# Last chunk of the input projection: sums of cb and gate tiles by accumulating transfers too, convolution and gating a block later, feed forward's sum cleared two blocks sooner

## The chip, the cores and the metric

The kernel runs on one core of a Trainium2 chip. The metric is the device time of one execution in microseconds. Before the change it is 1202.89 us, the median of three runs (1202.86 to 1203.3). The engines of the core are named as the profile names them: PE is TensorE (matrix products; PEld its weight loads), DVE is VectorE, ACT is ScalarE, POOL is GpSimd and SP is SyncE. Each runs its own list of instructions in order and waits on semaphores for the others.

## The reference, cut to what matters

One decoder layer on 256 rows of 2048 elements, float32. An input projection `proj = h @ w_in` gives eight parts; a gated short convolution (cb, cc, cx) and a gated linear attention (q, k, v, its decay, and the gate r) use them, the two results side by side go through `w_out`, and a feed-forward with its own convolution follows.

```python
def hybrid_mixer(h, w_in, conv_w, gate_w2, gate_b, gla_norm_w, w_out):
    proj = h @ w_in
    cb, cc, cx, q, k, v, r, a_lr = jnp.split(proj, splits, axis=-1)
    y_conv = cb * causal_dwconv3(cc * cx, conv_w)
    log_a = jax.nn.log_sigmoid(a_lr @ gate_w2 + gate_b) / GATE_TAU
    o = gla_chunked(q, k, v, log_a)
    o = rmsnorm(o, gla_norm_w) * jax.nn.silu(r)
    return jnp.concatenate([y_conv, y_gla], axis=-1) @ w_out

mod = c_act @ w_mod + b_mod
sh_m, sc_m, g_m, sh_f, sc_f, g_f = jnp.split(mod, 6)
h = rmsnorm(x, mix_pre_w) * (1 + sc_m) + sh_m
x = x + g_m * rmsnorm(hybrid_mixer(h, ...), mix_post_w)
h = rmsnorm(x, ffn_pre_w) * (1 + sc_f) + sh_f
x = x + g_f * rmsnorm(conv_ffn(h, ...), ffn_post_w)
```

cb, cc and cx are 1024 columns each, q and k 512 each, v and r 1024 each. The six rows of `mod` are products of one vector with a 2048 by 12288 matrix.

## The kernel before, in words

Every matrix product is made of three: both factors are split into a high part and the small rest, and high·high, high·low and low·high are added up in PSUM. For weights this costs, per tile, a load of `raw` (SP queue), a cast to `wh` on ACT (L140) and a subtraction to `wl` on DVE (L145).

The work is a list of units, each with one weight tile of about 1 MB. `drive` writes the order out by hand: for unit i first the steps in its list `early`, then the load and the cast of unit i+2, the `wl` of unit i+1, the steps in `pre`, the products of unit i on PE (after its first tile the steps in `inner`), the steps in `mid`, the evacuations of unit i−1, and the steps in `late`. What is written down first runs first on its engine, so these lists are the schedule.

The input projection goes over its contraction in four chunks. A chunk's units cover all output columns; sums over the chunks are kept in SBUF. In the first chunk a finished PSUM tile is copied there, in the second and third DVE adds PSUM to it. In the fourth, the last, there are two ways. By one, DVE adds as before (L477 for column tiles of 128x512, L494 for row tiles of 128x384 or 128x256). By the other, for the names in `BY_DMA` (cc, cx and v), ACT copies PSUM to a tile `hf` (L474, L491), of which there are three buffers, and POOL starts a DMA that adds `hf` into the sum in SBUF (L475, L492). Column pair 10, the first pair of cx1, is left out of the second way.

`tail` lists the last chunk's 18 units and then the 16 units of the out-projection, so tail[18] is the first of those. The chunk's order is k, v, cc/cx/cb (tail[6] to tail[14]) and the gate r (tail[15] to tail[17], three, three and two column tiles of each half, r0 and r1 being the two halves of the rows). The tables of numbers in the diff are places in `tail`:

- `CONV` puts the four pairs of the convolution: cc·cx (L668 on DVE), the first tap (L673 on ACT), four taps and the product with cb (L136 and L680 on DVE), and the split into high (L684 on ACT) and low (L688 on DVE).
- `SILU` puts the two halves of silu of r (L893 on ACT, after a table load).
- `GATE` puts, for the four heads, the product with the gate (`gated`, L868 on DVE, in `pre`), the transposes on PE (`turn`, L874, in `late`), and a unit later the scaled copies (L880 on ACT, L136 on DVE), which are the left factors of the out-projection's later units.

The linear attention's result comes out of PSUM by L861 (ACT) after its row norms (L401, L851).

An out unit is 24 products of 512 columns (L913, L914, L915) into four PSUM banks that stay in use over eight units; there are eight banks in all.

The rows of `mod` are summed on DVE, step by step, in a tile `macc` of 128x2048 (L136, one step per MB of `w_mod`). A sum begins on POOL with a memset of `macc` (L174) and a small DMA of the bias (L175). Its end is a product with ones on PE (L355, into four banks) which DVE takes from there (L360). `f1` is the sum for the feed-forward's shift and scale: 17 steps, of which the first is the begin, spread over early and mid places of units from `MODS[3]` = 48 (tail[7]) on; the units tail[12], [13], [16] and [17] are left out. L355 and L360 at about 375 us are of the sum before it, used after the out-projection.

Of the kernel before, what the change touches and what calls it, by code (L numbers as in the profile page):

```python
# [24 lines left out]
CHUNKS = (2, 4, 5, 5)  # L25
# [10 lines left out]
NBIG = 20  # L36
XLD = (4, 8)
NLD = (9, 13)
GATE = (18, 19, 20, 21)
SILU = (17, 18)  # L40
CONV = (9, 12, 13, 15)
MODS = (10, 22, 33, 48, 72)
CHUNK1 = 12
BUSY_TAIL = (12, 13, 16, 17)
BY_DMA = ("cc", "cx", "v")
F2_AT = (71, 74, 16)
FULL = ()
FULL1 = ()
# [19 lines left out]
def spread(steps, units, last=()):  # L68

    places = [p for u in units for p in ((u.early, u.mid, u.late) if u in last else (u.early, u.mid))]  # L70
    for i, f in enumerate(steps):
        places[i * len(places) // len(steps)].append(f)
# [31 lines left out]
def layer_kernel(ctx: ExitStack, tc, x, c, w_mod, b_mod, mix_pre_w, mix_post_w, w_in, conv_w, gate_w2, gate_b,  # L104
# [14 lines left out]
    def nm(s):  # L119
        uid[0] += 1  # L120
        return f"{s}_{uid[0]}"

    def slot(shape, dt=F32):
        return big.tile(shape, dt, tag="big", name=nm("big"))
# [7 lines left out]
    def raw_tile(shape):  # L132
        return wts.tile(shape, F32, tag="raw", name=nm("raw"), bufs=NRAW)

    def stt(o, a, s, b, op0=ALU.mult, op1=ALU.add):
        nc.vector.scalar_tensor_tensor(o, a, s, b, op0=op0, op1=op1)  # L136
# [24 lines left out]
    def mod_steps(s0, n, a, w, nj, lag=0):  # L161

        accs, cur, rows = [], {}, []

        def use(j, r):
            stt(cur["acc"], r, c_act[:, j:j + 1], cur["acc"])

        def begin():  # L170
            acc = cur["acc"] = (slot([P, n, w]) if n * w <= 1024 else
                                wts.tile([P, n, w], F32, tag="macc", name=nm("macc"), bufs=2))
            accs.extend(acc[:, s, :] for s in range(n))
            nc.gpsimd.memset(acc, 0.0)  # L174
            nc.gpsimd.dma_start(acc[0:1, :, :], b_mod_v[:, s0:s0 + n, a:a + w])  # L175

        def step(j):
            if j >= KT:
                use(*rows.pop(0))
                return  # L180
            m = nj if j < KT - nj or nj < 4 else 2
            if j % m == 0:
                cur["r"] = raw_tile([P, m, n, w])
                if m == 1:
                    nc.sync.dma_start(cur["r"][:, 0, :, :], w_mod_v[:, j, s0:s0 + n, a:a + w])
                else:
                    for s in range(n):
                        nc.sync.dma_start(cur["r"][:, :, s, :], w_mod_v[:, j:j + m, s0 + s, a:a + w])
            rows.append((j, cur["r"][:, j % m, :, :]))
            if j >= lag:  # L190
                use(*rows.pop(0))

        return accs, [begin] + [lambda j=j: step(j) for j in range(KT + lag)]
# [241 lines left out]
    def hf_tile():  # L435
        return wts.tile([P, 2, T], F32, tag="hf", name=nm("hf"), bufs=NHF)
# [24 lines left out]
    def evac(ci, pair, ps):  # L461

        name = names[pair // 2]
        if name not in proj:
            proj[name] = slot([P, 4, T])
        dst = proj[name][:, (pair % 2) * 2:(pair % 2) * 2 + 2, :]
        if pair not in written:
            written.add(pair)
            nc.scalar.activation(dst, ps, AF.Copy, scale=QS if name == "q" else 1.0)
        elif name == "q":  # L470
            stt(dst, ps, QS, dst)
        elif ci == len(CHUNKS) - 1 and name[:-1] in BY_DMA and pair != 10:
            away_sum = hf_tile()
            nc.scalar.copy(away_sum, ps)  # L474
            nc.gpsimd.dma_start(dst, away_sum, accum_op=ALU.add)  # L475
        else:
            nc.vector.tensor_add(dst, dst, ps)  # L477

    def evac_rows(ci, tiles, t, ps):
# [7 lines left out]
        if ci == 0:  # L487
            nc.scalar.copy(dst, ps)
        elif ci == len(CHUNKS) - 1 and name[:-1] in BY_DMA:
            away_sum = hf_tile().rearrange("p a t -> p (a t)")[:, :w]  # L490
# [64 lines left out]
    def in_units(ci):  # L555
# [18 lines left out]
        def unit(tiles, plain, by_parts=False):  # L574
# [72 lines left out]
            def fin():  # L647
                for p in dict.fromkeys(nt // 2 for nt in tiles):
                    done[p] = done.get(p, 0) + sum(nt // 2 == p for nt in tiles)
                    if done[p] == 2 and p not in keep:  # L650
                        evac(ci, p, banks[p])
# [10 lines left out]
    def conv_pair(i):  # L662

        s = slice((i % 2) * 2, (i % 2) * 2 + 2)

        def first():
            cb, cc, cx = (proj[n + str(i // 2)][:, s, :] for n in ("cb", "cc", "cx"))
            nc.vector.tensor_mul(cc, cc, cx)  # L668

        def tap():  # L670
            cc, cx = (proj[n + str(i // 2)][:, s, :] for n in ("cc", "cx"))
            for j in range(2):
                nc.scalar.activation(cx[:, j, :], cc[:, j, :], AF.Copy, scale=conv_c(2, 2 * i + j))  # L673

        def second():
            cb, cc, cx = (proj[n + str(i // 2)][:, s, :] for n in ("cb", "cc", "cx"))
            for tap, d in ((1, 1), (0, 2)):
                for j in range(2):
                    stt(cx[:, j, d:], cc[:, j, :T - d], conv_c(tap, 2 * i + j), cx[:, j, d:])
            nc.vector.tensor_mul(cb, cb, cx)  # L680

        def high_part():
            mts[i] = slot([P, 2, 2, T], F32R)
            nc.scalar.copy(mts[i][:, :, 0, :], proj["cb" + str(i // 2)][:, s, :])  # L684

        def third():
            cb = proj["cb" + str(i // 2)][:, s, :]
            nc.vector.tensor_sub(mts[i][:, :, 1, :], cb, mts[i][:, :, 0, :].bitcast(F32))  # L688

        return first, tap, second, high_part, third  # L690
# [199 lines left out]
    def gate_silu(g):  # L890
        for t in range(2):
            r = proj[f"r{t}"][:, g * 512:(g + 1) * 512]
            nc.scalar.activation(r, r, AF.Silu)  # L893
# [331 lines left out]
    allin = [u for c in chunks for u in c] + owait  # L1225
# [32 lines left out]
    for h in range(2):  # L1258
        owait[r0 + R0 + 1].mid.append(lambda h=h, f=ones_rows: f(h))
        owait[r0 + R0 + 2].late.append(lambda h=h, f=rows_used: f(h))  # L1260
    f1, fsteps = mod_steps(3, 2, 0, 1024, 1)
    spread(fsteps, [u for i, u in enumerate(allin) if MODS[3] <= i < MODS[4] and i - ends[2] not in BUSY_TAIL])
    for place, f in seconds:
        place.append(f)
# [29 lines left out]
    for g in range(2):  # L1294
        tail[SILU[g]].late.append(lambda g=g: gate_silu(g))
    for e in range(4):
        tail[GATE[e]].pre.append(lambda e=e: gated(e))
        tail[GATE[e]].late.append(lambda e=e: turn(e))
        tail[GATE[e] + 1].pre.append(lambda e=e: weighted(e))
        tail[GATE[e] + 1].late.append(lambda e=e: weighted_low(e))  # L1300
    for i, u in enumerate(CONV):
        first, tap, second, high_part, third = conv_pair(i)
# [220 lines left out]
def build(nc, tc_args=None, arrays=None):  # L1523
    import concourse.tile as _tile

    args = []
    for name, a in arrays.items():
        args.append(nc.dram_tensor(f"in_{name}_dram", a.shape, mybir.dt.from_np(a.dtype), kind="ExternalInput").ap())
    for i, (shape, dtype) in enumerate(_OUTS):
        args.append(nc.dram_tensor(f"out_{i}_dram", shape, getattr(mybir.dt, dtype), kind="ExternalOutput").ap())  # L1530
    with _tile.TileContext(nc, **(tc_args or {})) as tc:
        with tc.manual_schedule():
            layer_kernel(tc, *args)
# [13 lines left out]
```

## Time and profile before

| what | value |
|---|---|
| median of three runs | 1202.89 us (1202.86 to 1203.3) |
| the profiled execution | 1203.08 us |
| its span, from first to last instruction | 1201.1 us |
| busy in the span | PE 97%, DVE 78%, ACT 48%, POOL 4% |
| granted TensorE clock, mean | 0.998 |
| input projection's last chunk | about 250 to 344.7 us |
| out-projection's first product | 344.68 us |

The profile is one execution. A timeline row has the start, the duration, the engine, the line, the tiles and sizes, and in brackets the idle time just before it and what ended that. A row of the chain of waits has start, duration and the work or wait that it stands for; "issue" is time in which the engine waited for nothing that the profile shows. In the groups by line the count is followed by busy time, mean duration of one in ns, and idle time before with its releaser. Buffer numbers are left out of names: `big<-hf` is any of the accumulating transfers.

### The profile page before, as it was taken

The page shows a single profiled execution, that of the slowest core. Times are in us where ns is not written, and L with a number is a line of the kernel's source. Part 1 is how long each engine was busy: PE and PEld are TensorE (multiplying, and loading weights), DVE is VectorE, ACT ScalarE, POOL GpSimd, SP SyncE. Part 2 cuts the span into 40 slices and gives each one's busy share as a digit, 9 for nine tenths or more (in the row PEclk, how much of TensorE's full clock was granted, in tenths as well). Part 3 has the DMA queues.
Part 4 walks back from the last instruction along what each step waited for, and adds up shares of the span by engine and source line. Part 5 has one row for each costly group of instructions (what it writes and reads, how often), then busy time and mean ns, then how long its engine had stood idle before and what let it go on. Part 6 is the DMA issues. An engine that isn't in the chain of part 4 may idle for free.

```text
span 1201.1 us, 16724 instructions
## 1 busy us (share of the span) xinstructions
PE 1166.5 (97%) x6771; PEld 1027.6 (86%) x6771; DVE 939.5 (78%) x963; ACT 576.7 (48%) x671; POOL 47.8 (4%) x66
## 2 busy tenths in 40 slices
PE   3899999999999999999999999999999999999997
PEld 2799999999987888888888888888888888888885
DVE  6979999999999868984698979797976664545463
ACT  4663433463683556445455444544544544343442
POOL 3000110011101010000000000000000000000000
PEclk9999999999999999999999999999999999999999
DMA  9999999998899969995476777668563675555522
GB/s 340 387 361 378 331 383 393 388 330 272 240 341 372 367 248 333 378 369 212 168 260 213 258 259 249 223 243 293 201 236 140 228 263 201 185 202 184 207 73 71
DMA packets 129182, 323.62 MB, mean 269 GB/s; under 512 B 8550, under 2 KB 35894, under 8 KB 119377
## 3 DMA queue, kind: packets, MB, share of 16 engines
q1 hardware_dynamic: 124704, 312.63, 72.2%
q0 software_dynamic: 4256, 9.92, 3.0%
q8 instruction: 53, 0.87, 0.3%
q14 instruction: 25, 0.20, 0.0%
q10 hardware_dynamic: 144, 0.01, 0.0%
HBM read 315.45 MB, written 4.19 MB: 266 GB/s over the span
## 4 chain that ended last, share of the span: by engine, by line
PE 57%; issue 30%; DVE 5%; DMA 5%; ACT 1%; SPq 1%; POOL 1%; POOLq 0%; DVEq 0%; ACTq 0%
PE ps L1057 27%; PE ps L1059 14%; PE ps L913 3%; PE ps L915 3%; PE ps L914 3%; DVE wl L145 1%; DMA big<-hf 1%; PE ps L640 1%; PE ps L639 1%; DVE macc L136 1%; PE ps L638 1%; DMA raw<-in_w_mod_dram 1%; DMA big<-in_w_in_dram 1%; DMA raw<-in_w_in_dram 1%; DMA big<-in_w_mod_dram 1%
## 5 line engine op out<-in xcount | busy, mean ns | idle before, releaser
L140 ACT CAST wh<-raw 128x2048 fp32r<-128x2048 f32 (+2 forms) x200 | 366.3, 1833 | 498.3 <-PE ps L1057 187.3
L145 DVE TENSOR_TENSOR wl<-raw,wh 128x2048 fp32r<-128x2048 f32 (+2 forms) x200 | 437.4, 2190 | 144.7 <-ACT wh L140 144.6
L1057 PE MATMUL ps<-big,wh 128*128 128x512 f32 x1400 | 495.0, 399 | 0.0
L1059 PE MATMUL ps<-big,wl 128*128 128x256 f32 x1400 | 393.1, 281 | 0.0
L1057 PEld LDWEIGHTS ps<-big,wh 128*128 128x128 f32 x1400 | 263.0, 188 | 64.8
L1059 PEld LDWEIGHTS ps<-big,wl 128*128 128x128 f32 x1400 | 264.5, 189 | 0.0
L136 DVE SCALAR_TENSOR_TENSOR macc<-raw,c_act,macc 128x2048 f32<-128x2048 f32 (+1 forms) x96 | 199.3, 2076 | 4.5 <-DMA raw<-in_w_mod_dram 2.2
L913 PE MATMUL ps<-wh,big 128*128 128x512 f32 x456 | 178.4, 391 | 0.0
L915 PE MATMUL ps<-wh,big 128*128 128x512 f32 x456 | 177.5, 389 | 0.0
L914 PE MATMUL ps<-wl,big 128*128 128x512 f32 x456 | 177.5, 389 | 0.0
L640 PE MATMUL ps<-big,wl 128*128 128x256 f32 x504 | 143.3, 284 | 4.6 <-DVE wl L145 4.6
L638 PE MATMUL ps<-big,wh 128*128 128x256 f32 x504 | 143.8, 285 | 0.0
L639 PE MATMUL ps<-big,wh 128*128 128x256 f32 x504 | 142.6, 283 | 0.1
L640 PEld LDWEIGHTS ps<-big,wl 128*128 128x128 f32 x504 | 96.5, 192 | 5.9 <-DVE wl L145 5.8
L915 PEld LDWEIGHTS ps<-wh,big 128*128 128x128 f32 x456 | 85.6, 188 | 18.0
L913 PEld LDWEIGHTS ps<-wh,big 128*128 128x128 f32 x456 | 85.6, 188 | 17.9 <-issue 0.2
L914 PEld LDWEIGHTS ps<-wl,big 128*128 128x128 f32 x456 | 85.6, 188 | 17.6 <-issue 0.2
L639 PEld LDWEIGHTS ps<-big,wh 128*128 128x128 f32 x504 | 96.6, 192 | 0.3 <-DVE big L433 0.3
L638 PEld LDWEIGHTS ps<-big,wh 128*128 128x128 f32 x504 | 96.6, 192 | 0.4 <-ACT wh L140 0.3
L136 DVE SCALAR_TENSOR_TENSOR big<-big,fcw,big 128x254 f32<-128x254 f32 (+1 forms) x176 | 72.1, 475 | 0.0
L983 DVE TENSOR_TENSOR big<-big,ps 128x256 f32<-128x256 f32 x88 | 31.1, 415 | 46.5 <-ACT big L981 46.5
L604 PE MATMUL ps<-wl,big 128*128 128x384 f32 (+2 forms) x168 | 57.1, 340 | 1.2 <-DVE wl L145 1.2
(222 smaller groups left out, 914.0 us busy)
## 6 DMA issues: line engine op xcount, KB each, us to landing
raw<-in_w_up_dram SPq DMA_DIRECT2D x88, 1024.0 KB, 5.1
raw<-in_w_mod_dram SPq DMA_DIRECT2D x64, 1024.0 KB, 6.9
raw<-in_w_down_dram SPq DMA_DIRECT2D x44, 1024.0 KB, 4.8
raw<-in_w_in_dram SPq DMA_DIRECT2D x26, 960.0 KB, 8.0
raw<-in_w_mod_dram SPq DMA_DIRECT2D x32, 640.0 KB, 7.9
raw<-in_w_out_dram SPq DMA_DIRECT2D x16, 1024.0 KB, 7.5
raw<-in_w_in_dram SPq DMA_DIRECT2D x12, 1024.0 KB, 9.1
raw<-in_w_mod_dram SPq DMA_DIRECT2D x22, 512.0 KB, 8.4
```

Source lines behind the costliest of these rows:

```text
L136: nc.vector.scalar_tensor_tensor(o, a, s, b, op0=op0, op1=op1)
L140: nc.scalar.copy(hi, raw)
L145: nc.vector.tensor_sub(lo, raw, hi.bitcast(F32))
L604: nc.tensor.matmul(ps, ht[:, 0, :], w[1][:, kk, :], start=False, stop=kk == n - 1)
L638: nc.tensor.matmul(ps, w[0][:, kk, cs], ht[:, k % 2, 0, :], start=st, stop=False)
L639: nc.tensor.matmul(ps, w[0][:, kk, cs], ht[:, k % 2, 1, :], start=False, stop=False)
L640: nc.tensor.matmul(ps, w[1][:, kk, cs], ht[:, k % 2, 0, :], start=False, stop=sp)
L913: nc.tensor.matmul(ps, a[:, i, 0, ts_], w[0][:, kk, ns], start=st, stop=False)
L914: nc.tensor.matmul(ps, a[:, i, 0, ts_], w[1][:, kk, ns], start=False, stop=False)
L915: nc.tensor.matmul(ps, a[:, i, 1, ts_], w[0][:, kk, ns], start=False, stop=sp)
L1057: nc.tensor.matmul(pss[o], wh[:, kk, cs], h2[k // 2][:, k % 2, :, :], start=(first and kk == 0), stop=False)
L1059: nc.tensor.matmul(pss[o][:, 1, :], wl[:, kk, cs], h2[k // 2][:, k % 2, 0, :], start=False, stop=(last and kk == 3))
```

## The change

cb and r join the names whose last sums go by DMA, and pair 10 is no exception any more: five sums at L477 and six at L494 become a copy on ACT and a DMA of POOL each. The places of gating, silu and convolution move back by one unit each. The begin of `f1` (memset and bias) is taken out of the spread steps and put at the end of tail[5]; the remaining 16 steps are spread over the same places.

```diff
-GATE = (18, 19, 20, 21)
-SILU = (17, 18)
-CONV = (9, 12, 13, 15)
+GATE = (19, 20, 21, 22)
+SILU = (18, 19)
+CONV = (10, 13, 14, 16)
...
-BY_DMA = ("cc", "cx", "v")
+BY_DMA = ("cb", "cc", "cx", "v", "r")
...
-        elif ci == len(CHUNKS) - 1 and name[:-1] in BY_DMA and pair != 10:
+        elif ci == len(CHUNKS) - 1 and name[:-1] in BY_DMA:
             away_sum = hf_tile()
             nc.scalar.copy(away_sum, ps)
             nc.gpsimd.dma_start(dst, away_sum, accum_op=ALU.add)
...
-    f1, fsteps = mod_steps(3, 2, 0, 1024, 1)
+    f1, (f_begin, *fsteps) = mod_steps(3, 2, 0, 1024, 1)
+    allin[MODS[3] - 2].late.append(f_begin)
     spread(fsteps, [u for i, u in enumerate(allin) if MODS[3] <= i < MODS[4] and i - ends[2] not in BUSY_TAIL])
```

Three places show how the order moves. The first is ACT at the turn from the last chunk to the out-projection. `big_511` and `big_513` are the sums of r0 and r1, `ps_...` a PSUM tile, `hf_...` one of the three buffers, `wh_...` a cast weight tile. Before:

```order
L684 CAST big_3445<-big_337 128x2x256
L140 CAST wh_3449<-raw_3447 128x2048
L893 ACT_TABLE_LOAD
L893 ACTIVATE big_511<-big_511 128x512
L893 ACTIVATE big_513<-big_513 128x512
L140 CAST wh_3495<-raw_3493 128x2048
```

With the change:

```order
L491 COPY hf_3447<-ps_3342 128x384
L491 COPY hf_3450<-ps_3358 128x384
L673 ACTIVATE big_483<-big_415,sv 128x256 x2
L140 CAST wh_3459<-raw_3457 128x2048
L491 COPY hf_3500<-ps_3415 128x384
L491 COPY hf_3503<-ps_3431 128x384
L684 CAST big_3506<-big_337 128x2x256
L140 CAST wh_3510<-raw_3508 128x2048
L491 COPY hf_3545<-ps_3468 128x256
L491 COPY hf_3548<-ps_3484 128x256
L893 ACT_TABLE_LOAD
L893 ACTIVATE big_511<-big_511 128x512
```

Six copies now stand among the casts and ahead of the silu, and the silu is one cast later. hf_3503 is the fourth of the six copies; with three buffers it takes the place of hf_3447.

The second place is PE in the out-projection, where the products of the mod rows (L355) stand. Before, the list goes from an out unit to L355 and to the next out unit:

```order
L913 MATMUL ps_3504<-wh_3588,big_3547 128x512
L914 MATMUL ps_3504<-wl_3636,big_3547 128x512
L915 MATMUL ps_3504<-wh_3588,big_3547 128x512
L355 MATMUL ps_3710<-macc_1910,ones 128x512
L355 MATMUL ps_3712<-macc_1910,ones 128x512
L355 MATMUL ps_3714<-macc_1910,ones 128x512
L355 MATMUL ps_3716<-macc_1910,ones 128x512
L913 MATMUL ps_3501<-wh_3634,big_3592 128x512
```

With the change:

```order
L915 MATMUL ps_3517<-wh_3598,big_3602 128x512
L355 MATMUL ps_3725<-macc_1910,ones 128x512
L355 MATMUL ps_3727<-macc_1910,ones 128x512
L355 MATMUL ps_3729<-macc_1910,ones 128x512
L355 MATMUL ps_3731<-macc_1910,ones 128x512
L874 MATMUL ps_3735<-ident,big_3405 128x128
L874 MATMUL ps_3735<-ident,big_3410 128x128
L874 MATMUL ps_3735<-ident,big_3405 128x128
L874 MATMUL ps_3735<-ident,big_3410 128x128
L913 MATMUL ps_3514<-wh_3647,big_3651 128x512
```

The transposes of the fourth head (L874) stood one out unit ahead of L355 and now stand right behind it.

The third place is POOL at v's last transfers (`big_563`, `big_565`). Before:

```order
L492 DMA big_563<-hf_2656 128x384
L492 DMA big_565<-hf_2659 128x384
L492 DMA big_563<-hf_2735 128x256
L492 DMA big_565<-hf_2738 128x256
L174 MEMSET macc_2744 128x2048
L175 DMA macc_2744<-in_b_mod_dram 1x2x1024
```

With the change:

```order
L492 DMA big_563<-hf_2656 128x384
L492 DMA big_565<-hf_2659 128x384
L174 MEMSET macc_2662 128x2048
L175 DMA macc_2662<-in_b_mod_dram 1x2x1024
L492 DMA big_563<-hf_2738 128x256
L492 DMA big_565<-hf_2741 128x256
```

The memset and the bias now go ahead of v's third pair of transfers.

## The prediction, on record before the changed kernel's time was known

> **What bounds the kernel now.** First the busy times on the page.
>
> ```profile
> PE 1166.5 (97%) x6771; PEld 1027.6 (86%) x6771; DVE 939.5 (78%) x963; ACT 576.7 (48%) x671; POOL 47.8 (4%) x66
> ```
>
> TensorE is busy 97% of 1201.1 us, so only the places where it stands still can be gained. The view by windows of 10 us over the last chunk and the start of the out-projection (columns: PE, PEld, DVE, ACT and POOL busy, with counts; granted clock; DMA share; GB/s) shows where these are.
>
> ```profile
> 290.00:300.00 10.00, 9.54 (x81) 9.34 (x80) 10.00 (x11) 3.64 (x5) 0.00 (x0) 1.00 0.70 240
> 310.00:320.00 10.00, 8.10 (x69) 7.89 (x69) 9.97 (x15) 6.73 (x13) 0.85 (x1) 1.00 0.99 314
> 340.00:350.00 10.00, 9.86 (x59) 8.54 (x57) 9.96 (x11) 9.67 (x15) 0.00 (x0) 1.00 0.80 289
> 350.00:360.00 10.00, 9.55 (x46) 7.54 (x45) 10.00 (x13) 6.34 (x8) 0.00 (x0) 1.00 0.99 384
> ```
>
> In each, DVE is full while PE is not, at a granted clock of 1.00. The timeline of PE gives the four stalls to a hundredth.
>
> ```profile
> 294.26 0.28 PE L639 MATMUL ps<-big,wh 128*128 128x256 f32 x1
> 295.00 0.39 PE L640 MATMUL ps<-big,wl 128*128 128x256 f32 x1 [0.46 <-DVE wl L145]
> ...
> 314.96 0.28 PE L639 MATMUL ps<-big,wh 128*128 128x256 f32 x1
> 317.14 0.39 PE L640 MATMUL ps<-big,wl 128*128 128x256 f32 x1 [1.90 <-DVE wl L145]
> 317.37 0.28 PE L638 MATMUL ps<-big,wh 128*128 128x256 f32 x1
> 317.49 0.28 PE L639 MATMUL ps<-big,wh 128*128 128x256 f32 x1
> ...
> 340.50 0.34 PE L604 MATMUL ps<-wl,big 128*128 128x384 f32 x1
> 340.98 0.39 PE L602 MATMUL ps<-wh,big 128*128 128x256 f32 x1
> ...
> 344.68 0.40 PE L913 MATMUL ps<-wh,big 128*128 128x512 f32 x1
> ...
> 349.92 0.39 PE L915 MATMUL ps<-wh,big 128*128 128x512 f32 x1
> 350.75 0.88 PE L874 MATMUL ps<-ident,big 128*128 128x128 f32 x4 [0.45 <-DVE big L868]
> 351.39 0.48 PE L913 MATMUL ps<-wh,big 128*128 128x512 f32 x1
> ```
>
> Back to back, 256 columns follow each other by 0.12 us (317.37 to 317.49). The first two steps take 0.74 and 2.18, so 0.62 and 2.06 are lost, both to wl (L145) coming late from DVE. By the same reckoning 0.31 is lost at 340.98 (0.48 against some 0.17 for 384 columns), and 0.60 at 350.75 (0.83 against 0.23: a unit's 24 matmuls take 349.92 + 0.23 − 344.68 = 5.47). Together **3.6 us**: a ceiling, 0.3% of the time.
>
> **The change part by part.** I call S the start of the out-projection (344.68 before) and follow the terms in the order of the program.
>
> *Work leaving DVE.* The groups by line between 200 and 440 us (count, then busy time and mean ns):
>
> ```profile
> L494 DVE TENSOR_TENSOR big<-big,ps 128x384 f32<-128x384 f32 (+1 forms) x14 | 6.3, 491 | 0.0
> L477 DVE TENSOR_TENSOR big<-big,ps 128x512 f32<-128x512 f32 x8 | 5.3, 676 | 0.4 <-PE ps L640 0.4
> L491 ACT COPY hf<-ps 128x384 f32<-128x384 f32 (+1 forms) x6 | 2.4, 439 | 3.5 <-DMA big<-hf 3.5
> L868 DVE TENSOR_TENSOR big<-big,big 128x256 f32<-128x256 f32 x8 | 3.0, 420 | 0.0
> L893 ACT ACTIVATE big<-big 128x512 f32<-128x512 f32 x4 | 2.3, 624 | 1.7 <-DVE big L494 1.7
> ```
>
> Five sums at L477 and six at L494 leave DVE: 5×0.68 + 6×0.49 = 6.3 us by durations. ACT, idle 3 to 6 us in each window but that of 340 to 350, takes eleven copies, POOL eleven DMA starts. Of these sums two stand ahead of the 2.06 stall, and the convolution's L668, four taps and L680 in its neighbourhood go a block later; I take both stalls on wl as gone. The 0.31 stall ends with L861's first results on ACT, which come sooner because L673 and its wait no longer stand ahead (rows below). The 0.60 stall goes because its transposes go two units later. Term **−3.6 us**; the floor of the gain is zero, if DVE uses the freed time to wait for landings.
>
> *f1's sum cleared sooner.* The chain of waits, at v's last transfers and the memset:
>
> ```profile
> 266.08 7.12 DMA big<-hf
> ...
> 273.58 0.38 ACT hf L491
> 273.96 0.28 issue
> 274.25 0.85 POOL big L492
> 275.10 1.82 POOL macc L174
> ...
> 280.39 2.24 issue
> ```
>
> DVE stood 2.24 us at 280.39, its first sum into macc waiting for the bias behind this memset. Memset and bias now go ahead of v's third transfers, so the bias is down some 7 us sooner and that wait goes. The first macc sum now stands ahead of a wl instead of behind it, and its duration (2.35 in the rows further below) is about the 2.24 saved. PE needs that wl at about the time it then comes: **+0.1**, at most the 0.6 that PE lost to wl at 295. The spread has one step less, because the begin step stands apart; the work is the same.
>
> *The gate's rows by transfer.* This is the long chain. The views of ACT and of the DMA (issues, KB each, median us to landing; the smallest, median and largest of all thirteen):
>
> ```profile
> 337.49 0.91 ACT L673 ACTIVATE big<-big,sv 128x256 f32<-128x256 f32 x2 [1.10 <-DVE big L668]
> 340.10 3.01 ACT L861 ACTIVATE big<-ps,grs 128x256 f32<-128x256 f32 x8
> ...
> big<-hf POOLq DMA_DIRECT2D x4, 192.0 KB, 7.6
> DMA to landing us min/median/max: 3.9/7.0/9.4
> ```
>
> L861 ends at 343.1, or S−1.6. Without the 1.10 wait it ends near S−2.5. The first two copies of the gate (r0, then r1, first three tiles) stand right behind it: a copy of 0.44 and 0.28 to POOL put the first transfer's start at S−1.7. There are three hf buffers. The fourth copy (r1, second three tiles) therefore waits for the first transfer to land, exactly as v's copy did at 273.58: from 266.08 to the next start at 274.25 that hop took 8.17. So the fourth transfer starts at S+6.5, lands 7.6 later at S+14.1, and the silu over both rows (L893, second of its pair) may only then begin: 0.38 for the wake and start as at 273.58, 0.62 of silu, 0.42 of L868, make S+15.6 with 0.1 of signal. Gating a block later lets PE do two units first, 2×5.47, to S+11.0. PE stands **+4.6 us** at the first transposes (L874). What ACT holds behind the blocked copy are the casts of two more blocks of w_out (L140); what DVE holds behind L868 are the next macc sum and wl. PE waits for the same L868 anyway, so these delays are inside the 4.6.
>
> Put generally the stall is (the two landings together) − 10.1. With 3.9 for each it is nothing; with 9.4 for each it is 8.7. I take 7.12 and 7.6, the rows nearest in size and in DMA load: the windows at 310 and 350 have a DMA share of 0.99, that between them 0.80.
>
> [...]
>
> *The fourth transposes behind the mod rows.* Rows of PE and DVE in the out stage of before:
>
> ```profile
> 374.78 3.60 PE L355 MATMUL ps<-macc,ones 128*128 128x512 f32 x8
> 377.81 0.79 PE L913 MATMUL ps<-wh,big 128*128 128x512 f32 x1
> ...
> 351.61 2.35 DVE L136 SCALAR_TENSOR_TENSOR macc<-raw,c_act,macc 128x2048 f32<-128x2048 f32 x1
> 353.87 2.29 DVE L145 TENSOR_TENSOR wl<-raw,wh 128x2048 fp32r<-128x2048 f32 x1
> ...
> 357.53 2.34 DVE L136 SCALAR_TENSOR_TENSOR macc<-raw,c_act,macc 128x2048 f32<-128x2048 f32 x1
> 379.08 2.48 DVE L360 TENSOR_TENSOR big<-ps,big 128x512 f32<-128x512 f32 x4
> ```
>
> The four sums of the out-projection hold four PSUM banks and L355's products the other four. Before, the last L874 ran a unit ahead of L355; now it comes directly behind and needs a bank, which the first L360 on DVE gives back. Call E the end of the stall above. A unit of PE with its transposes is 5.47 + about 0.5, so three of them and L355 (3.03, from 374.78 to 377.81) bring PE there at E+21.0. DVE does macc, wl, L868 and the weighted part per unit in 5.92 (351.61 to 357.53), three times, then a wl (2.2), a macc (2.26) and one L360 (0.62): E+22.9, and 0.1 of signal. **+2.0 us**. It is there only because DVE starts level with PE at E; DVE so far ahead that L360 needn't wait would need 2 us of slack at L868. Bounds: 0 and 2.4.
>
> Sum: −3.6 + 0.1 + 4.6 + 2.0 = **+3.1 us**. At 97% over the whole span PE has no slack behind it that would give this back. The profiled execution took 1203.08 (span 1201.1 and 2.0 around it), 0.2 above the median of 1202.89. Its 1206.2 is 1206.0 for the median.
>
> **The rivals.** *The transfers land early.* At 4.5 us each (9.0 together) PE never waits at the first L874, DVE has 1.1 in hand and the bank costs 0.9: −3.6 + 0.1 + 0.9 = −2.6, time 1200.3, faster. For it: the shortest landing, 3.9. Against: it needs under 5.05 each, two thirds of the median. [...]
>
> *Middle landings.* At 6.2 each: stall 2.3, bank 2.0, sum +0.8, time 1203.7, no change that can be told. For it: the spread of the thirteen is as wide as that. Against: the load of DMA around S.
>
> *The transfers meet the loads of w_out.* The chain of waits has one such, near the end of the chunk, and the timeline of DVE the wait that it made:
>
> ```profile
> 327.77 8.90 DMA big<-hf
> ...
> 336.76 0.69 DVE L668 TENSOR_TENSOR big<-big,big 128x512 f32<-128x512 f32 x1 [1.59 <-DMA big<-hf]
> ```
>
> With 8.9 for each the stall is 17.8 − 10.1 = 7.7 and the sum +6.2: 1209.1. For it: this is the latest landing before S, in a window as full. Against: it carried 256 KB.
> [...] The trace shows only that landings vary from 3.9 to 9.4, not why.
>
> *The change doesn't do what it says:* DVE loses the sums but waits instead for cb to land at L680, and the 3.6 stay. With the terms of the gate that is +6.7, 1209.6. For it: the 1.59 that L668 waits for a landing, just above. Against: the convolution goes a block later, which gives each transfer some 5 us more.
>
> **How the numbers follow.** Chances: forecast 0.42, early landings 0.20, middle 0.20, meeting w_out 0.12, cb late 0.06. A measurement of this kernel can tell about 0.2%, or 2.4 us, from no change: 1200.5 to 1205.3. Early landings are nearly all below that (0.18 faster, 0.02 not). The middle case, and a quarter of the forecast's (landings a little under 7), are inside: 0.20 + 0.11 + 0.02 = 0.33. Slower is 0.49. The range runs from the early case's middle, 1200.3, to 1209.6; it leaves out half of the early case and a part of the long landings, some 2 in 10. The forecast's own range is 1204.5 to 1207.5.
>
> **What would show it.** In the changed kernel's profile: no wait of L640 on wl between 285 and 320; L491 with twelve copies and one of the later ones waiting for the landing of hf; L893 waiting for big<-hf instead of L494; PE waiting at L874 for L868 for some 4.6 us about 10 us into the out-projection, and some 2 us more right behind L355. If the landings of the gate's transfers are near 5 us, or the first L893 waits for nothing, the third and fourth terms are wrong. If L640 still waits for wl, or DVE idles at L668 and L680, the first is wrong. If the last L874 follows L355 without a gap although the first one stood, the bank's term is wrong.

## The result, and the profile after

The changed kernel takes 1206.46 us (median of seven runs, 1205.97 to 1208.1) against 1202.86 us before (seven runs): a ratio of 1.0031, 95% interval 1.0019 to 1.0042. It is slower by 3.6 us; forecast were 3.1. The profiled execution took 1206.61 us, its span is 1204.8.

The page of the changed kernel, part 1, and its view by windows of 10 us (columns as before the change):

```profile
PE 1167.3 (97%) x6771; PEld 1028.6 (85%) x6771; DVE 934.9 (78%) x952; ACT 580.9 (48%) x682; POOL 57.3 (5%) x77
...
290.00:300.00 10.00, 10.00 (x88) 10.00 (x88) 10.00 (x11) 3.41 (x5) 0.85 (x1) 1.00 0.88 233
310.00:320.00 10.00, 10.00 (x87) 10.00 (x86) 9.75 (x14) 6.99 (x15) 3.42 (x4) 1.00 1.08 309
350.00:360.00 10.00, 5.71 (x24) 4.52 (x23) 5.30 (x4) 5.77 (x9) 2.85 (x4) 0.90 1.04 318
```

DVE has eleven operations less, ACT and POOL eleven more. The hole at 310 to 320 us, where PE had been busy 8.10 of 10, is closed. A new one is open at 350 to 360: PE 5.71 of 10, at a mean granted clock of 0.90. The timeline of PE shows what it is.

```profile
287.67 0.28 PE L639 MATMUL ps<-big,wh 128*128 128x256 f32 x1
288.40 0.39 PE L640 MATMUL ps<-big,wl 128*128 128x256 f32 x1 [0.46 <-DVE wl L145]
...
342.44 0.40 PE L913 MATMUL ps<-wh,big 128*128 128x512 f32 x1
...
353.35 0.27 PE L874 MATMUL ps<-ident,big 128*128 128x128 f32 x1
357.90 0.78 PE L874 MATMUL ps<-ident,big 128*128 128x128 f32 x3 [4.29 <-DVE big L868]
358.34 0.77 PE L913 MATMUL ps<-wh,big 128*128 128x512 f32 x1
358.91 0.63 PE L914 MATMUL ps<-wl,big 128*128 128x512 f32 x1
359.33 0.63 PE L915 MATMUL ps<-wh,big 128*128 128x512 f32 x1
...
361.47 0.41 PE L914 MATMUL ps<-wl,big 128*128 128x512 f32 x1
361.72 0.40 PE L915 MATMUL ps<-wh,big 128*128 128x512 f32 x1
...
377.25 3.60 PE L355 MATMUL ps<-macc,ones 128*128 128x512 f32 x8
380.91 0.66 PE L874 MATMUL ps<-ident,big 128*128 128x128 f32 x4
```

The out-projection starts at 342.44 instead of 344.68, 2.2 us sooner. Then PE waits at the first transposes from 353.35 to 357.90. The first seven products behind that wait follow each other by 0.42 to 0.43 us (358.91 to 359.33) where 0.23 is usual, some 1.4 us in all. From L355 to the last transposes it is 3.66 us, where 3.03 would do: 0.6 lost. The feed-forward's first product comes 3.2 us later than before, the span is 3.7 longer; where the other 0.5 arises was not traced.

The chain that makes the long wait, in the timelines of ACT, POOL and DVE:

```profile
339.75 0.90 ACT L491 COPY hf<-ps 128x384 f32<-128x384 f32 x2
343.09 0.53 ACT L491 COPY hf<-ps 128x384 f32<-128x384 f32 x1
347.44 0.48 ACT L491 COPY hf<-ps 128x384 f32<-128x384 f32 x1 [3.82 <-DMA big<-hf]
356.76 0.63 ACT L893 ACTIVATE big<-big 128x512 f32<-128x512 f32 x1 [4.02 <-DMA big<-hf]
...
340.56 1.75 POOL L492 DMA_DIRECT2D big<-hf  x2 [10.28 <-ACT hf L491]
348.21 0.86 POOL L492 DMA_DIRECT2D big<-hf  x1 [3.44 <-ACT hf L491]
...
357.42 0.43 DVE L868 TENSOR_TENSOR big<-big,big 128x256 f32<-128x256 f32 x1 [4.22 <-ACT big L893]
...
380.16 2.48 DVE L360 TENSOR_TENSOR big<-ps,big 128x512 f32<-128x512 f32 x4
```

The first of r's transfers starts at 340.56. The fourth copy of r waits 3.82 us for it to land, since there are three hf buffers, and its own transfer starts at 348.21. The silu waits 4.02 for that one, L868 for the silu and PE for L868. The last row is the product on DVE that gives back the bank for PE's transposes at 380.91.

### The profile page after: what moved, and what is told of

Its sections match the earlier page's. It is cut to its first block, busy times and chain, and to the rows that moved or that the text cites. A ratio compares the mean times of both kernels' runs of the same rounds, so it can differ in the third digit from the quotient of the medians.

```text
span 1204.8 us, 16755 instructions
## 1 busy us (share of the span) xinstructions
PE 1167.3 (97%) x6771; PEld 1028.6 (85%) x6771; DVE 934.9 (78%) x952; ACT 580.9 (48%) x682; POOL 57.3 (5%) x77
## 4 chain that ended last, share of the span: by engine, by line
PE 82%; DVE 5%; DMA 5%; issue 4%; ACT 1%; SPq 1%; POOL 1%; DVEq 0%; POOLq 0%; ACTq 0%
PE ps L1057 27%; PE ps L1059 14%; PE ps L914 8%; PE ps L915 8%; PE ps L913 8%; PE ps L640 3%; PE ps L639 3%; PE ps L638 3%; DMA raw<-in_w_mod_dram 2%; PE ps L603 2%; PE ps L602 2%; PE ps L604 2%; DVE macc L136 1%; DVE wl L145 1%; DMA big<-in_w_mod_dram 1%
## 5 line engine op out<-in xcount | busy, mean ns | idle before, releaser
L640 PE MATMUL ps<-big,wl 128*128 128x256 f32 x504 | 143.1, 284 | 2.7 <-DVE wl L145 2.7
L640 PEld LDWEIGHTS ps<-big,wl 128*128 128x128 f32 x504 | 96.6, 192 | 3.6 <-DVE wl L145 3.5
```

The lines of the kernel that those rows point to most:

```text
L640: nc.tensor.matmul(ps, w[1][:, kk, cs], ht[:, k % 2, 0, :], start=False, stop=sp)
```

## The experiments

Each kernel was timed in five rounds (5 to 11 executions) beside the kernel before, whose medians were 1202.82, 1203.05 and 1203.09 us in the three groups of four runs. Ratios are to those, with 95% intervals.

**r's sums back on DVE.**

```diff
-BY_DMA = ("cb", "cc", "cx", "v", "r")
+BY_DMA = ("cb", "cc", "cx", "v")
```

> The changed kernel with r's last sums back on DVE (L494); gating, silu and all else as changed. Theory (two transfers in a row, tied by the three hf buffers, hold silu and so the first transposes): the 4.3 us wait of PE at the first L874 goes, with it the 1.4 us in which PE ran at a lower granted clock behind it; the wait behind L355 may stay at 0.6 or grow to 2. DVE takes six sums of 0.48 back, in a stretch (320 to 350 us) where it idles some 4 us. Time 1200.5 to 1202.5. Rival (the extra copies and transfers in the chunk, cb's too, take the time by contention): at least 1205.

Measured: 1199.55 us, ratio 0.9974 (0.9964 to 0.9984). It is faster than before, by more than was expected of it. The timeline of PE in this run:

```profile
341.49 0.40 PE L913 MATMUL ps<-wh,big 128*128 128x512 f32 x1
...
352.40 0.60 PE L874 MATMUL ps<-ident,big 128*128 128x128 f32 x4
...
370.21 3.60 PE L355 MATMUL ps<-macc,ones 128*128 128x512 f32 x8
373.96 0.66 PE L874 MATMUL ps<-ident,big 128*128 128x128 f32 x4 [0.16 <-DVE big L360]
```

PE comes to the first transposes 10.9 us into the out-projection and does not wait. The gap between L355 and the last L874 stays at 0.7. So six transfers of r cost 6.9 us of 1206.46, and everything else in the change together gains 3.3.

**Only r1 back on DVE.**

```diff
-        elif ci == len(CHUNKS) - 1 and name[:-1] in BY_DMA:
+        elif ci == len(CHUNKS) - 1 and name[:-1] in BY_DMA and name != "r1":
             away_sum = hf_tile().rearrange("p a t -> p (a t)")[:, :w]
```

> The changed kernel with only r1's last sums back on DVE; r0 keeps its three transfers, one for each hf buffer. Theory (it is the hop over the third buffer that is late): no copy of r waits for a landing of r, the second r0 transfer starts near the out-projection's start and lands some 8 us behind it, ahead of PE's 11; the wait at the first L874 is under 1 us; time 1200.5 to 1202.5, as with all of r on DVE. Rival (one transfer of r is late enough by itself, or DMA load is what counts): a wait of 2 us or more stays, time 1203.5 or more.

Measured: 1202.52 us, ratio 0.9995 (0.9986 to 1.0004), just outside what the theory allowed. For the long wait the theory holds: without the hop over the third buffer no copy of r waits, and the first L874 goes without a stop at 352.62. (This run also halves the number of r's transfers; more buffers with all six were not tried.) But rows of ACT, DVE and PE show what the rest of the time went to:

```profile
354.67 1.15 ACT L893 ACTIVATE big<-big 128x512 f32<-128x512 f32 x2 [2.02 <-DMA big<-hf]
...
358.39 0.88 DVE L136 SCALAR_TENSOR_TENSOR big<-ps,sv,big 128x256 fp32r<-128x256 f32 x2 [1.54 <-ACT big L880]
...
376.22 1.11 PE L874 MATMUL ps<-ident,big 128*128 128x128 f32 x4 [2.23 <-DVE big L360]
376.99 0.78 PE L913 MATMUL ps<-wh,big 128*128 128x512 f32 x1
377.56 0.63 PE L914 MATMUL ps<-wl,big 128*128 128x512 f32 x1
377.99 0.63 PE L915 MATMUL ps<-wh,big 128*128 128x512 f32 x1
```

The second silu waits 2.02 us on ACT for the last transfer. Behind it on ACT stand a cast and L880. DVE waits 1.54 for L880, comes that much later to L360, and PE stands 2.23 at the last transposes, with slow products (0.43 apart) behind. So in this run transfers that land in time for the first head are late for what is queued behind the second. This is one execution, of 1203.51 us; the eleven spread from 1199.63 to 1204.21, the eight with all of r on DVE only from 1199.21 to 1200.73. What the shorter ones paid is not shown.

**Silu and gating one unit later still.**

```diff
-GATE = (19, 20, 21, 22)
-SILU = (18, 19)
+GATE = (20, 21, 22, 23)
+SILU = (19, 20)
```

> The changed kernel with silu and gating yet one unit later. Theory (the end of the chain is fixed by the landings and not by where the gating stands): PE has 5.9 us more work ahead of the first L874, so a wait of 4.3 is covered; the granted clock stays at 1.00; the wait behind L355 is 0 to 2; time 1200.5 to 1202.5. Rival (the landings come later too when PE and the loads of w_out run on, or other work behind it becomes late, such as the scaled copies for the fifth out unit): a wait at L874 or at L913 of 2 us or more stays, 1203.5 or more.

Measured: 1203.13 us, ratio 0.9998 (0.9989 to 1.0007). The long wait is covered, as expected, but the time is above the forecast. PE's rows, and the window behind them:

```profile
357.50 0.60 PE L874 MATMUL ps<-ident,big 128*128 128x128 f32 x4
...
375.26 0.66 PE L874 MATMUL ps<-ident,big 128*128 128x128 f32 x4 [2.29 <-DVE big L360]
...
376.00:378.00 2.00, 2.00 (x7) 1.56 (x6) 2.00 (x5) 0.79 (x2) 0.16 (x1) 0.64 1.04 346
```

The bank's wait is now 2.29 us, at the third head's transposes, and the clock is down to 0.64 behind it. The theory holds for the first wait only; "0 to 2" behind L355 was too low, and the clock, expected to stay at 1.00, fell.

**The same, with the mod rows one unit later.**

```diff
-R0 = 1
+R0 = 2
```

> The changed kernel with silu and gating one unit later and the mod rows two units... that is, R0 raised by one: the mod rows (L355, L360) one out unit later as well. With gating alone one unit later the first wait was gone but PE stood 2.9 us between L355 and L874 and ran some 3 us at a lower clock behind it, 1203.1. Theory: at that gating the last transposes still stand behind L355's bank by their place (third ahead, fourth behind), so with L355 a unit later only the third and fourth are in question, and the wait shrinks to under 1 us; time 1199 to 1200.5, which would show that r by transfer costs nothing where it is waited for late enough. Rival (DVE is behind for another reason): 1202 or more.

Measured: 1202.51 us, ratio 0.9994 (0.9985 to 1.0003). PE at the last transposes:

```profile
380.83 0.66 PE L874 MATMUL ps<-ident,big 128*128 128x128 f32 x4 [1.84 <-DVE big L360]
```

The expectation was wrong: with both one unit later, the last transposes stand right behind L355 again, and the wait there (1.84 us, in an execution of 1201.13) is of the same kind. So it was not shown that r by transfer can be had for nothing.

**cb and pair 10 back on DVE.**

```diff
-BY_DMA = ("cb", "cc", "cx", "v", "r")
+BY_DMA = ("cc", "cx", "v", "r")
...
-        elif ci == len(CHUNKS) - 1 and name[:-1] in BY_DMA:
+        elif ci == len(CHUNKS) - 1 and name[:-1] in BY_DMA and pair != 10:
```

> The changed kernel with cb's and pair 10's last sums back on DVE; r by transfer as changed. Theory (cb's transfers are a gain, of the wl waits in the chunk): some of the 2.4 us gained before the out-projection is lost again, the wait at the first L874 stays at 4 to 5; time 1206.5 to 1209. Rival (cb's transfers delay those of r, or contend with the loads): the wait at L874 falls by 1 us or more and the time is below 1205.5.

Measured: 1207.22 us, ratio 1.0033 (1.0021 to 1.0046), not to be told from the changed kernel's 1.0031. The timeline of PE:

```profile
341.96 0.40 PE L913 MATMUL ps<-wh,big 128*128 128x512 f32 x1
...
357.77 0.90 PE L874 MATMUL ps<-ident,big 128*128 128x128 f32 x3 [4.46 <-DVE big L868]
```

The long wait stays. But the out-projection starts at 341.96, not later than with cb by transfer. The time fits the theory, the reason that it gave (waits on wl that come back) does not.

**All eleven transfers undone.** What stays are the moved convolution, gating and silu and the sooner begin of f1's sum.

```diff
-BY_DMA = ("cb", "cc", "cx", "v", "r")
+BY_DMA = ("cc", "cx", "v")
...
-        elif ci == len(CHUNKS) - 1 and name[:-1] in BY_DMA:
+        elif ci == len(CHUNKS) - 1 and name[:-1] in BY_DMA and pair != 10:
```

> The changed kernel with all eleven new transfers undone (cb, pair 10 and r on DVE again); the moved convolution, gating, silu and the sooner begin of f1's sum stay. Theory A (the sums that leave DVE remove the stalls on wl): without them the 2 us stall on wl near 315 is back, the time is 1201.5 to 1203. Theory B (the moved convolution and the sooner begin remove them, as the start of the out-projection at 341.96 with cb on DVE suggests): the time is 1199 to 1200.5, that of r on DVE alone (1199.55).

Measured: 1200.5 us, ratio 0.9981 (0.9972 to 0.9989). PE in this run:

```profile
342.01 0.40 PE L913 MATMUL ps<-wh,big 128*128 128x512 f32 x1
...
375.44 0.66 PE L874 MATMUL ps<-ident,big 128*128 128x128 f32 x4 [1.14 <-DVE big L360]
```

Theory B: the large stall on wl goes without a single sum leaving DVE; of those on wl only one of 0.6 us is left, at 287.7, as in the changed kernel. What DVE does ahead of that wl, before:

```profile
310.68 2.34 DVE L136 SCALAR_TENSOR_TENSOR macc<-raw,c_act,macc 128x2048 f32<-128x2048 f32 x1
...
315.61 1.48 DVE L145 TENSOR_TENSOR wl<-raw,wh 128x1280 fp32r<-128x1280 f32 x1
```

In this run:

```profile
275.36 2.35 DVE L136 SCALAR_TENSOR_TENSOR macc<-raw,c_act,macc 128x2048 f32<-128x2048 f32 x1 [0.75 <-issue]
...
302.92 2.35 DVE L136 SCALAR_TENSOR_TENSOR macc<-raw,c_act,macc 128x2048 f32<-128x2048 f32 x1
...
313.36 1.48 DVE L145 TENSOR_TENSOR wl<-raw,wh 128x1280 fp32r<-128x1280 f32 x1
```

DVE now stands idle for 0.75 us ahead of its first macc sum, where it had been 2.24, and by 305.3 it has done the sum that stood at 310.68 right ahead of the wl before. That wl comes 2.2 us sooner. Beside the run with r alone on DVE (0.9974) the transfers of cb are worth 0.9 us by the medians, and the intervals overlap.

**Of that, the sooner begin undone too.**

```diff
-    f1, (f_begin, *fsteps) = mod_steps(3, 2, 0, 1024, 1)
-    allin[MODS[3] - 2].late.append(f_begin)
+    f1, fsteps = mod_steps(3, 2, 0, 1024, 1)
```

> The run without the eleven new transfers (1200.5), with the begin of f1's sum put back among the spread steps too: of the change only the moved convolution, gating and silu are left. Theory B1 (the sooner begin removes the stall on wl near 315: one sum into macc, 2.3 us of DVE, leaves the stretch from 299 to 316, for it is done at 276 where DVE stood idle): the stall is back with 1.5 to 2 us, time 1201.5 to 1203. Theory B2 (the moved convolution removes it): no stall near 315, time 1199.5 to 1201.

**Of that, the convolution put back instead**, with the sooner begin kept.

```diff
-CONV = (10, 13, 14, 16)
+CONV = (9, 12, 13, 15)
```

> The run without the eleven new transfers (1200.5), with the convolution put back a unit sooner: of the change only the begin of f1's sum, gating and silu are left. Theory B1: no stall of more than 0.7 near 315, time 1200 to 1201.5. Theory B2: the stall is back with 1.5 to 2 us, time 1202 to 1203.

Measured: 1202.74 us (0.9997, 0.9988 to 1.0006) without the sooner begin, 1202.28 us (0.9995, 0.9987 to 1.0004) without the moved convolution. The waits of PE, first without the sooner begin, then without the moved convolution:

```profile
PE ps L640 <- DVE wl L145: 2.0, 2, 1.5
PE ps L874 <- DVE big L360: 1.5, 1, 1.5
```

```profile
PE ps L640 <- DVE wl L145: 1.2, 3, 0.5
PE ps L602 <- ACT big L861: 0.6, 1, 0.6
```

The large stall comes back (1.5 us) without the sooner begin: B1. Without the moved convolution it does not, but two small ones on wl (0.3 and 0.4 us of waiting, at 310 and 320) and the one behind L861 stand there, and that run missed its forecast by 0.8. Each of the two alone is not to be told from before, both together gain 2.5 us. Gating and silu are a unit later in all three runs, so their part in this is not separated.

**The mod rows one unit later**, in the changed kernel.

```diff
-R0 = 1
+R0 = 2
```

> The changed kernel with the mod rows (L355, L360) one out unit later, so that the last transposes run ahead of L355 again; nothing else. Theory (PE stands at the last L874 for the bank which the first L360 gives back): the gap of 0.6 us between L355 and L874 goes and no other takes its place; the first wait of 4.3 and the lower clock behind it stay; time 1205.2 to 1206.3. Rival (it is DVE's lateness as such): a wait of the same size appears at another place, time as changed, 1206.5.

Measured: 1205.92 us, ratio 1.0026 (1.0015 to 1.0037). The gap of 0.6 is gone and no other took its place: the last L874 starts at 377.91, L355 a unit later at 383.84. 0.5 us less, as expected; it cannot be told from the changed kernel by the intervals, and the profiled execution was the longest of the seven (1207.08).

**Products in the place of the wait.** 60 products of 128 columns, whose results nobody uses, ahead of the first transposes.

```diff
+        if e == 0:
+            def filler():
+                ps = bank([P, P])
+                for i in range(NFILL):
+                    nc.tensor.matmul(ps, ones_r, ones_r, start=i == 0, stop=i == NFILL - 1)
+            tail[GATE[e]].late.append(filler)
         tail[GATE[e]].late.append(lambda e=e: turn(e))
```

> The changed kernel with 60 more products of 128 columns (results unused, some 4 us) on PE ahead of the first transposes, where PE stood 4.3 us. Theory C (the lower granted clock of 0.81 to 0.85 behind that wait comes from PE having stood): the clock stays at 1.00 there, the seven products at 0.43 us instead of 0.23 behind it return to 0.23 and PE comes 1.4 us sooner to L355. Theory D (DVE's chain from the first L868 to the first L360 sets the end of this stretch whatever PE does): the wait behind L355 grows from 0.6 to 2.0 by that same 1.4 and the time stays at 1206 to 1207. If C holds and D doesn't, 1205.1.

**42 of them, and the mod rows one unit later.** The same edit with `NFILL = 42` and `R0 = 2`.

> The changed kernel with the mod rows one out unit later (1205.9 so far) and 42 products of 128 columns on PE ahead of the first transposes; 60 of them took 6.81 us and outlasted the wait by 1.6, 42 take 4.8. Theory C (the lower clock behind the wait costs time of its own, which the wait behind L355 hid so far): with that wait out of the way the time falls by the clock's part, 1.4 to 2.0, to 1204 to 1204.6, at a granted clock of 1.00. Theory D (DVE sets the end of the stretch in any case): it stays at 1205.5 to 1206.5.

Measured: 1207.15 us (1.0035, 1.0023 to 1.0048) with 60, and 1204.34 us (1.0011, 1.0002 to 1.002) with 42 and the mod rows later. First the run with 60 (its lines stand one further; the last row is a window), then two windows: the run with the mod rows later and no filler, and the same with 42.

```profile
352.74 6.81 PE L1304 MATMUL ps<-ones_r 128*128 128x128 f32 x60
...
359.39 0.62 PE L875 MATMUL ps<-ident,big 128*128 128x128 f32 x4
...
380.75 0.66 PE L875 MATMUL ps<-ident,big 128*128 128x128 f32 x4
...
355.00:360.00 5.00, 5.00 (x46) 5.00 (x46) 3.50 (x3) 3.23 (x4) 0.00 (x0) 1.00 1.06 383
```

```profile
355.00:360.00 5.00, 2.38 (x7) 2.02 (x8) 2.86 (x3) 3.52 (x5) 0.00 (x0) 0.62 1.03 320
```

```profile
355.00:360.00 5.00, 5.00 (x34) 4.54 (x34) 3.70 (x3) 3.14 (x4) 0.00 (x0) 1.00 1.07 372
```

With 60 the clock stays at 1.00, which is theory C; but they took 6.8 us instead of the 4 expected and outlast the wait: DVE starts the awaited product at 356.50, and the transposes, 0.48 behind it in the changed kernel, start at 359.39. So that run says little of what the clock is worth. PE's last transposes come at 380.75, against 380.91 in the changed kernel. That looks like theory D but does not show it: the wait behind L355 is 0.5 us and not the 2.0 that D expects, for the late transposes cost PE what the clock had cost it, and DVE itself waited 0.86 us for the scaled copies behind them. With 42, which end in time, and L355 out of the way the time falls from 1205.92 to 1204.34, 1.6 us, the clock's part as forecast. The two intervals overlap by a little. 42 with L355 in its place, which would test theory D, was not run.

**The best of these**: r on DVE, the mod rows one unit later, all else as changed.

```diff
-BY_DMA = ("cb", "cc", "cx", "v", "r")
+BY_DMA = ("cb", "cc", "cx", "v")
...
-R0 = 1
+R0 = 2
```

> Candidate for the best: the changed kernel with r's sums on DVE (1199.55) and the mod rows one out unit later. The gap of 0.7 between L355 and L874 should go: time 1198.6 to 1199.3. If DVE's lateness shows elsewhere instead, 1199.5.

Measured: 1199.04 us, ratio 0.9968 (0.9955 to 0.998), faster than the kernel before and than the changed one; from r on DVE alone (0.9974) the intervals do not tell it. PE has no wait over 0.5 us left in this stretch.

## Why the prediction was right, and where its steps were not

**The gate's rows by transfer, +4.6: right.** The first transfer started 1.9 us ahead of the out-projection (forecast 1.7), the hop took 7.65 (8.17), from the fourth transfer's start to the silu were 8.55 (7.6 + 0.38), and PE stood 4.55 (4.6). With r on DVE the wait is gone, with r0 alone by transfer too; together with the 3.82 us that the fourth copy waits, this makes the hop over the third buffer its cause. A fourth buffer was not tried. One small slip: L861's end at 343.1 less the 1.10 is S−2.7 and not S−2.5, which gives the 1.9 that came. Landings of the size of v's, not of the shortest in the trace, were the right choice.

**The bank behind L355, +2.0: the end was right, the way there not.** The wait there is only 0.6. The step that failed is "bring PE there at E+21.0": it had PE run at full clock behind a wait of 4.6. PE lost 1.4 by its clock and so met DVE later; both together are the 2.0. The reckoning of DVE held: it has no idle time from L868 at 357.42 to L360 at 380.16, and PE's last transposes start at E+23.0 (357.90 and 380.91), as forecast. That they would have come no sooner with PE at full clock follows from these rows and was not run by itself. The run with 42 agrees with a clock that costs 1.6 of its own once the bank is out of the way.

**The work leaving DVE, −3.6: size nearly right, by luck for its largest part.** Of the stalls named, 2.06, 0.31 and 0.60 went. For 0.31 and 0.60 the reasons hold: with the convolution at its old places PE waits for L861 again, and with gating a unit later (the prediction says two) and r on DVE the first transposes do not wait. For the 2.06 the step that failed is to count on the sums, "of these sums two stand ahead of the 2.06 stall". With every one of them back on DVE it is gone all the same. What closes it without them is the sooner begin of f1's sum, which brings one macc sum of 2.3 us into the stretch where DVE stood idle; the moved convolution, which the prediction had named too, takes smaller ones. The prediction had booked that begin as a cost of 0.1 because it looked only at the wl next to it, not at the sum missing later on. Whether the sums alone would have closed the stall was not run.

**f1's begin, +0.1 to 0.6:** the upper bound came true. PE loses 0.61 at 288.40 behind the macc sum that now stands ahead of a wl, in the place of the 0.62 at 295 before. By the prediction's own sign, no wait of L640 between 285 and 320, this is a small miss.

**The rivals.** Early landings, middle landings and those of 8.9 are answered by the hop and the landing above: 16.2 us together, where the forecast's own terms make 8.17 + 7.6 + 0.38 = 16.15. r's four transfers of 192 KB landed after 7.0 us in the median. DVE waiting for cb at L680 does not occur: no L680 waits for a landing, and L668's wait in the changed kernel is 0.2 us.

## What to carry to other kernels

Moving a sum from a full engine to a copy and an accumulating transfer takes work off that engine, here 0.49 to 0.68 us a sum. But here it put some 8 us between the result and its reader (8.55 from the fourth transfer's start to the silu), and with three buffers for six transfers in a row a hop of 7.65 us ahead of that. The five sums of cb and of pair 10, read later, cost DVE at most one wait of 0.2 us for a landing; the six of r, read at the end of the stage, cost 6.9 us of the time. And where an engine is full, ask first whether some of its work can be moved into a hole that it has elsewhere: here one early clear of an accumulator and a convolution moved by a unit (gating and silu too) gained 2.5 us with all eleven sums on DVE, while with the sums moved too the kernel was 3.6 slower than before.

## What the runs showed of the hardware

The forecast had no term for PE's clock at all, and in the changed kernel it cost 1.4 us. Behind 4.55 us of standing, seven products of 512 columns took 0.43 us each instead of 0.23; behind 2.23 us (r1 on DVE) and 2.29 (gating later) products at 0.43 follow too. Behind 1.84 and 1.47 us (gating and mod rows later; the run without the sooner begin) the windows show 1.00. Three windows show the clock where it is low: the changed kernel, gating later, and the mod rows later.

```profile
358.10:361.40 3.30, 3.30 (x10) 2.69 (x9) 3.30 (x2) 3.12 (x4) 0.00 (x0) 0.50 1.06 400
```

```profile
376.60:379.90 3.30, 3.30 (x10) 2.52 (x9) 3.30 (x5) 0.19 (x1) 0.00 (x0) 0.50 1.05 345
```

```profile
356.30:363.00 6.70, 5.38 (x14) 4.33 (x15) 5.86 (x6) 5.99 (x7) 0.00 (x0) 0.50 0.98 351
```

It is 0.50 over the 3.30 us of the first two windows and over the 6.70 us of the third. In the changed kernel the 3.30 us ahead of the window show 1.00 and those behind it 0.99; with gating later 374 to 376 us and 380 to 382 show 1.00. Its fall was not tied to the wait's end: in the changed kernel the window at 0.50 begins 0.2 us behind that (357.90), with gating later PE had been working for some 1.3 us again (from 375.26), and with the mod rows later the window begins at 356.30 while PE still stood (to 357.62). Nor was what it cost the same: the products at 0.43 reach from 358.91 to 361.47 in the changed kernel, from 358.75 to 363.01 with the mod rows later. One trace of each run does not show how short a wait can lower it.
